# A decoder layer on one core: the pair's last norms in fewer slabs, their additions of squares on GpSimd, and half tiles and embedding weights stored two to a tile

## The chip, the core and the metric

The kernel runs on one core of a Trainium2 chip. The core has a matmul engine (PE, with its weight loads as PEld), a vector engine (DVE), a scalar engine (ACT), GpSimd (POOL) and a queue engine that issues most DMAs (SP). The metric is the device time of one execution in microseconds. The kernel before takes 1129.64 us (median of 3 runs, 1128.06 to 1129.97).

## The reference, cut to what matters

One layer of a decoder over 1,056 tokens (1,024 of a prompt and 32 samples), model width 1,024. What the change touches is the channel part, the last norm and the per-layer embedding:

```python
    x = x + _rms(mix, n_mix_post)
    f = _rms(x, n_ffn_pre)
    f = (jax.nn.silu(f @ w_gate) * (f @ w_up)) @ w_down
    x = x + _rms(f, n_ffn_post)
    x = x + jax.nn.sigmoid(x @ w_ple_gate) * (p @ w_ple)
```

`_rms` divides by the root of the mean square over the 1,024 features and multiplies by a gain. `w_gate` and `w_up` are 1,024 x 2,816, `w_ple` is 256 x 1,024. All is fp32.

## The kernel before

**Numbers and tokens.** Activations lie with the features on partitions and the tokens along a row. The 1,056 tokens form three groups of 352: groups 0 and 1 ("the pair") and group 2 ("the one"). Every fp32 operand is split in two: ACT casts the high part (L171), DVE subtracts it to get the low part (L172). A product is three matmuls (high by high, high by low, low by high; L126).

**The channel part.** It walks over 11 slabs of 256 hidden features, for the one and for the pair apart: six slabs for the one, eleven for the pair, then the last five for the one. For the one a weight tile takes 24 matmuls in one go (`direct`). For the pair, `seven` computes the two-by-two block product of a pair of weight tiles and the two groups with seven products of 12 matmuls rather than eight: it needs sums of the weights, made in place by four GpSimd operations of 128x512 (`w_sums`, L1012) and split like any weight into `sh`/`sl`, and sums of the activations, T1 to T4, each one GpSimd subtraction of 128x1408 (`t_sum`, L971). A slab's down products (6 matmuls each, `down`) are added on DVE to `o` (L1117), and run after the first gate product of the next slab.

**The end.** After the last slab of a group `last_down` also squares `o` on ACT and adds the squares up on DVE (`squares_into`, L802 and L803). `x2_steps` then makes the norm: a sum over partitions by matmuls with the reciprocal root (`rstd_steps`), the scaling (L1141), the gain and the residual (L1144), and the split of the result. For the pair `pair_steps` does this for groups 0 and 1, makes T1 to T4 from the results, and loads and splits the embedding input p of both groups (`pl_load`, L1156). The embedding then runs four pairs of output tiles (`ple_pair`), each a `seven` whose four results go through a sigmoid and are each followed by `embed`: 6 matmuls with `w_ple` and p, a product on DVE (L1212), an addition (L1214) and a DMA out. The down products of the one's last slab lie between the first pair and the second. Eight single output tiles of the one follow (`ple_one`, in the order `LATE`).

**What sets the order.** Each engine runs its instructions in the order of the program's list, and each instruction waits for what it needs. Two things are paced by hand. Weights are a list `ITEMS` in order of use; `need(k)` makes items up to four ahead: a DMA by SP into a ring of three raw tiles (`wr`), then a split into a ring of eight tiles (`wp`, shown as `wh`, `wl`, `sh`, `sl`). Kinds of items are "direct" (a whole tile), "half" (only the second half of a tile is needed as it is) and "sums" (the pair of tiles just loaded). The norms' steps are generators driven by `turn(n)`, called after n matmuls: a step yields (load, wait), and the next one is written into the program after `load / share` plus `wait` further matmuls. The chains of the pair and the one start at the end of `downs`.

**Names in the rows.** `b` is a PSUM bank (there are eight), `pl` the split p, `fh`/`fl` the split activations, `hid` the split hidden features, `a` the raw p, `x` the residual of a group with `x1d` and `x2d` its copies in DRAM, `xm` the residual read back for the embedding, `acc` the sum of squares, `yo` an output tile.

Of the kernel before, what the change touches and what calls it, by code (L numbers as in the profile page):

```python
# [61 lines left out]
def trunk_kernel(  # L62
# [167 lines left out]
    def direct_item(src, shape):  # L230
        return item("direct", add_plan(src, shape))

    def half_item(src):
        return item("half", add_plan(src, [P, KC, P]))
# [23 lines left out]
    for i in range(KC // 2):  # L258
        wp = direct_item(w_ple[i // 2], [P, 2, 512]) if i % 2 == 0 else WP2[-1][0]
        jg = direct_item(w_pg[2 * i], [P, KC, P])  # L260
        ju = half_item(w_pg[2 * i + 1])
        WP2.append((wp, jg, ju, item("sums", jg, ju)))
        if i == 0:
            WD[-1] = dn_items(len(WALK) - 1)
    LATE = (*range(4, KC), *range(4))
    for m in LATE:
        if m == 0:
            wp = direct_item(w_ple[0], [P, 2, 512])
        WPE[m] = wp, direct_item(w_pg[m], [P, KC, P])

    made = {}

    def need(k, ahead=LOOK):

        for i in range(len(made), min(k + ahead + 1, len(ITEMS))):
            kind, js = ITEMS[i]
            if kind == "direct":
                w_split(js[0])
                made[i] = pairs[js[0]]
            elif kind == "half":  # L280
                w_load(js[0])
                hl = w_tile([P, 4, P], "wh"), w_tile([P, 4, P], "wl")
                split(*hl, raws[js[0]][:, 4:8, :])
                made[i] = hl
            else:
                made[i] = w_sums(*(raws[ITEMS[j][1][0]] for j in js))
            for kind, js in ITEMS[i + 1 : i + 3]:
                if kind != "sums":
                    w_load(js[0])
        return made[k]  # L290
# [49 lines left out]

    def sum_halves(sqs, g):

        a, b = sqs
        fix(ve.tensor_tensor(a, a, b, op=ALU.add))
        fix(ve.tensor_tensor(a[:, 0:2, :], a[:, 0:2, :], a[:, 2:4, :], op=ALU.add))
        acc = acc_tile(g)
        fix(ve.tensor_tensor(acc, a[:, 0, :], a[:, 1, :], op=ALU.add))
        return acc
# [447 lines left out]

    def squares_into(acc_g, src, first):
        if first:
            se.activation(acc_g, src, AF.Square)
        else:  # L800
            sq = tmp(src.shape[-1], "sq")
            se.activation(sq, src, AF.Square)  # L802
            ve.tensor_tensor(acc_g, acc_g, sq, op=ALU.add)  # L803

# [110 lines left out]
    def ffn_steps(g):  # L915
# [7 lines left out]
        yield 0, 13  # L923
        acc2 = sum_halves(ys[g], g)
        yield 20, 6
        r = yield from rstd_steps(acc2)
# [200 lines left out]
    def last_down(n, m, g):  # L1127
        down(n, m, g)
        if m == 0:
            acc3[g] = acc_tile(g)  # L1130
        squares_into(acc3[g], os_[g][m // 4][:, m % 4, :], m == 0)

# [31 lines left out]
    def pair_steps():  # L1164
        for g in (0, 1):
            yield from x2_steps(g, pair_operand)
        for name in ("T1", "T2", "T4", "T3"):
            t_sum(name, x27, x2[0], x2[1], flat(os_))
            yield 20, 0
        for g in (0, 1):  # L1170
            pl_load(g)
            yield 6, 0

# [6 lines left out]
    def downs(n):  # L1180
# [6 lines left out]
        if n == LAST[0]:  # L1187
            share[0] = 0.35
            chain(pair_steps(), 19)
        if n == LAST[2]:  # L1190
            chain(one_steps(), 19)

# [11 lines left out]
    def embed(wp, xm, m, g, sg):  # L1204

        wh, wl = need(wp)
        ph, pl = pls[g]
        cols = slice((m % 4) * P, (m % 4 + 1) * P)
        pp = bank()
# [53 lines left out]
def _layout(i):  # L1263
# [29 lines left out]
        "w_pg": tiles(i["w_ple_gate"][0]),  # L1293
        "w_ple": i["w_ple"][0].reshape(2, P, 2, 512).transpose(2, 1, 0, 3),
        "gains": gains,
# [40 lines left out]
```

## Time and profile before

| | |
|---|---|
| median of 3 runs | 1129.64 us |
| the profiled execution | 1132.07 us, its span 1130.1 us, mean granted clock 0.992 |
| PE busy | 1105.7 us, 98% of the span |
| DVE busy | 828.6 us, 73% |
| ACT busy | 480.8 us, 43% |
| POOL busy | 233.1 us, 21% |
| DMA | 125.25 MB in packets, mean 111 GB/s |

The span is from the first instruction to the last; the execution's time lies 2 us above it. In the rows of an engine the first number is the start, the second the length, both in us, and in brackets stands how long the engine was idle before and what ended it. Matmuls are pipelined, so a row of 0.32 us starts every 0.16 us. In a table by stretches each engine has its busy time and, in brackets, its instructions; the granted clock is 1.00 at full speed.

The last stage of the profile in its chain of waits ends in one run of PE, and the outputs behind it:

```profile
1075.49 50.15 PE b L126 x304
1125.73 0.53 DVE sg L1212
1126.29 0.52 DVE yo L1214
```

### The profile page before, as it was taken

The page shows a single profiled execution, that of the slowest core. Times are in us where ns is not written, and L with a number is a line of the kernel's source. Part 1 is how long each engine was busy: PE and PEld are TensorE (multiplying, and loading weights), DVE is VectorE, ACT ScalarE, POOL GpSimd, SP SyncE. Part 2 cuts the span into 40 slices and gives each one's busy share as a digit, 9 for nine tenths or more (in the row PEclk, how much of TensorE's full clock was granted, in tenths as well). Part 3 has the DMA queues.
Part 4 walks back from the last instruction along what each step waited for, and adds up shares of the span by engine and source line. Part 5 has one row for each costly group of instructions (what it writes and reads, how often), then busy time and mean ns, then how long its engine had stood idle before and what let it go on. Part 6 is the DMA issues. An engine that isn't in the chain of part 4 may idle for free. (4 is left out here: it accounts for less than half of the span.)

```text
span 1130.1 us, 17901 instructions
## 1 busy us (share of the span) xinstructions
PE 1105.7 (98%) x7099; PEld 1088.3 (96%) x7099; DVE 828.6 (73%) x1314; ACT 480.8 (43%) x832; POOL 233.1 (21%) x180
## 2 busy tenths in 40 slices
PE   9999999999999999999999999999999999968998
PEld 8999988899999999999999999999999999968898
DVE  5767478877979966566767767767767888977763
ACT  6423277665645533523323323323325544534331
POOL 0045132100001413123123123122130001422400
PEclk9999999999999999999999999999999999989999
DMA  8121311642643422222222222212215355452451
GB/s 285 57 69 43 119 48 36 205 145 94 220 143 113 135 100 83 76 75 75 75 75 76 80 71 77 88 60 86 83 57 173 119 212 180 155 186 87 134 182 58
DMA packets 41844, 125.25 MB, mean 111 GB/s; under 512 B 4869, under 2 KB 15397, under 8 KB 41761
## 3 DMA queue, kind: packets, MB, share of 16 engines
q1 hardware_dynamic: 40432, 122.35, 32.0%
q10 hardware_dynamic: 1328, 1.77, 0.5%
q8 instruction: 56, 0.92, 0.3%
q14 instruction: 28, 0.22, 0.1%
HBM read 111.11 MB, written 12.99 MB: 110 GB/s over the span
## 5 line engine op out<-in xcount | busy, mean ns | idle before, releaser
L171 ACT CAST wh<-wr 128x1024 fp32r<-128x1024 f32 (+1 forms) x177 | 171.7, 971 | 254.9 <-PE b L126 182.1
L172 DVE TENSOR_TENSOR wl<-wr,wh 128x1024 fp32r<-128x1024 f32 (+1 forms) x177 | 214.5, 1218 | 65.2 <-ACT wh L171 59.5
L126 PE MATMUL b<-hid,wh 128*128 128x352 f32 x1056 | 252.1, 322 | 0.0
L126 PE MATMUL b<-fh,wh 128*128 128x352 f32 x728 | 236.1, 324 | 1.6 <-DVE o L1117 1.6
L126 PE MATMUL b<-fh,wl 128*128 128x352 f32 x728 | 234.0, 321 | 0.0
L126 PE MATMUL b<-fl,wh 128*128 128x352 f32 x728 | 234.0, 321 | 0.0
L126 PEld LDWEIGHTS b<-hid,wh 128*128 128x128 f32 x1056 | 182.5, 188 | 0.1
L126 PE MATMUL b<-hid,wl 128*128 128x352 f32 x528 | 169.1, 320 | 0.0
L1012 POOL TENSOR_TENSOR wr<-wr 128x512 f32<-128x512 f32 x52 | 70.8, 1362 | 412.6 <-DVE wl L172 385.6
L126 PEld LDWEIGHTS b<-fh,wh 128*128 128x128 f32 x728 | 137.3, 189 | 1.9 <-DVE o L1117 1.9
L126 PEld LDWEIGHTS b<-fl,wh 128*128 128x128 f32 x728 | 137.7, 189 | 0.0
L126 PE MATMUL b<-fh,sh 128*128 128x352 f32 x416 | 135.1, 325 | 2.3 <-ACT sh L171 2.3
L126 PEld LDWEIGHTS b<-fh,wl 128*128 128x128 f32 x728 | 137.0, 188 | 0.0
L126 PE MATMUL b<-fh,sl 128*128 128x352 f32 x416 | 134.1, 322 | 1.3 <-DVE sl L172 1.3
L126 PE MATMUL b<-fl,sh 128*128 128x352 f32 x416 | 133.9, 322 | 0.0
L1117 DVE TENSOR_TENSOR o<-o,b 128x352 f32<-128x352 f32 x240 | 112.4, 515 | 15.9 <-PE b L126 15.9
L126 PE MATMUL b<-h,wh 128*128 128x352 f32 x480 | 107.4, 330 | 1.0 <-ACT h L379 1.0
L172 DVE TENSOR_TENSOR sl<-wr,sh 128x1024 fp32r<-128x1024 f32 x52 | 63.5, 1222 | 56.1 <-ACT sh L171 56.1
L126 PEld LDWEIGHTS b<-hid,wl 128*128 128x128 f32 x528 | 98.9, 187 | 0.0
L171 ACT CAST sh<-wr 128x1024 fp32r<-128x1024 f32 x52 | 53.3, 1048 | 93.1 <-POOL wr L1012 67.8
L126 PEld LDWEIGHTS b<-h,wh 128*128 128x128 f32 x480 | 83.4, 192 | 2.5 <-ACT h L379 1.7
L126 PEld LDWEIGHTS b<-fh,sh 128*128 128x128 f32 x416 | 78.5, 189 | 2.9 <-ACT sh L171 2.9
(165 smaller groups left out, 1702.2 us busy)
## 6 DMA issues: line engine op xcount, KB each, us to landing
wr<-in_w_gu_dram SPq DMA_DIRECT2D x88, 512.0 KB, 3.2
wr<-in_w_dn_dram SPq DMA_DIRECT2D x44, 512.0 KB, 3.6
wr<-in_w_pg_dram SPq DMA_DIRECT2D x16, 512.0 KB, 3.8
x<-in_x_dram SPq DMA_DIRECT2D x6, 704.0 KB, 7.7
x1d<-x SPq DMA_DIRECT2D x6, 704.0 KB, 3.4
x<-x1d SPq DMA_DIRECT2D x6, 704.0 KB, 5.4
out_y_dram<-yo SPq DMA_DIRECT2D x24, 176.0 KB, 2.7
wr<-in_w_out_b_dram SPq DMA_DIRECT2D x8, 512.0 KB, 3.3
```

The source lines that it names most:

```text
L126: ins = te.matmul(*args, **kw)
L171: fix(se.copy(hi, src))
L172: fix(ve.tensor_tensor(lo, src, hi.bitcast(F32), op=ALU.subtract))
L1012: ge.tensor_tensor(out, a, b, op=op)
L1117: ve.tensor_tensor(o, o, v, op=ALU.add)
```

## The change

Four things change.

1. A half tile's two parts go into one `wp` tile (`two_in_one`), so a "half" item takes one place of the ring of eight and not two.
2. `w_ple` is laid out as four tiles of 256 columns, one for each pair of output tiles, not two of 512. Each is an item of the new kind "small", its two parts in one `wp` tile, and stands in `ITEMS` behind the pair's sums; before, it stood ahead of the pair's first weight, for two pairs at once. The one's tiles take them in the order 6, 7, 0 to 5, so that the last pair's can be used again.
3. `pair_steps` loads and splits p first and not last; the steps of T1 to T4 yield (15, 10) and not (20, 0); the pair's chain runs at share 0.5 and not 0.35 ("fewer slabs"); the one's chain starts after 40 matmuls and not 19.
4. The additions of squares in the last slab of the pair (14 of 128x352), and the three additions of `sum_halves` in the first norms of groups 0 and 1, go from DVE to GpSimd; the step behind `sum_halves` yields (0, 45) there.

PE has the same 6,856 instructions in both lists; DVE has 1,301 and not 1,317, ACT 781 and not 779, POOL 206 and not 186, SP 254 and not 250.

```diff
+    def small_item(src):
+        return item("small", add_plan(src, [P, 2, 256]))
...
-        wp = direct_item(w_ple[i // 2], [P, 2, 512]) if i % 2 == 0 else WP2[-1][0]
         jg = direct_item(w_pg[2 * i], [P, KC, P])
         ju = half_item(w_pg[2 * i + 1])
-        WP2.append((wp, jg, ju, item("sums", jg, ju)))
+        js = item("sums", jg, ju)
+        WP2.append((small_item(w_ple[i]), jg, ju, js))
...
-    LATE = (*range(4, KC), *range(4))
+    wp = WP2[-1][0]
+    LATE = (6, 7, *range(6))
     for m in LATE:
-        if m == 0:
-            wp = direct_item(w_ple[0], [P, 2, 512])
+        if m < 6 and m % 2 == 0:
+            wp = small_item(w_ple[m // 2])
...
+    def two_in_one(shape):
+        t = w_tile([P, 2, shape[1] * shape[2]], "w2")
+        return tuple(t[:, h, :].rearrange("p (a b) -> p a b", a=shape[1]) for h in range(2))
...
-                hl = w_tile([P, 4, P], "wh"), w_tile([P, 4, P], "wl")
+                hl = two_in_one([P, 4, P])
                 split(*hl, raws[js[0]][:, 4:8, :])
                 made[i] = hl
+            elif kind == "small":
+                w_load(js[0])
+                hl = two_in_one([P, 2, 256])
+                split(*hl, raws[js[0]])
+                made[i] = hl
...
-    def sum_halves(sqs, g):
+    def sum_halves(sqs, g, eng=ve):
...
-    def squares_into(acc_g, src, first):
+    def squares_into(acc_g, src, first, eng=ve):
...
-            ve.tensor_tensor(acc_g, acc_g, sq, op=ALU.add)
+            eng.tensor_tensor(acc_g, acc_g, sq, op=ALU.add)
...
-        acc2 = sum_halves(ys[g], g)
-        yield 20, 6
+        acc2 = sum_halves(ys[g], g, ve if g == 2 else ge)
+        yield (20, 6) if g == 2 else (0, 45)
...
-        squares_into(acc3[g], os_[g][m // 4][:, m % 4, :], m == 0)
+        squares_into(acc3[g], os_[g][m // 4][:, m % 4, :], m == 0, ve if g == 2 else ge)
...
     def pair_steps():
         for g in (0, 1):
+            pl_load(g)
+        for g in (0, 1):
             yield from x2_steps(g, pair_operand)
         for name in ("T1", "T2", "T4", "T3"):
             t_sum(name, x27, x2[0], x2[1], flat(os_))
-            yield 20, 0
-        for g in (0, 1):
-            pl_load(g)
-            yield 6, 0
+            yield 15, 10
...
-            share[0] = 0.35
+            share[0] = 0.5
             chain(pair_steps(), 19)
         if n == LAST[2]:
-            chain(one_steps(), 19)
+            chain(one_steps(), 40)
...
-        cols = slice((m % 4) * P, (m % 4 + 1) * P)
+        cols = slice((m % 2) * P, (m % 2 + 1) * P)
...
-        "w_ple": i["w_ple"][0].reshape(2, P, 2, 512).transpose(2, 1, 0, 3),
+        "w_ple": i["w_ple"][0].reshape(2, P, 4, 256).transpose(2, 1, 0, 3),
```

Three places of the order. First SP's queue, where the weights of the first embedding pair are asked for. Before (`in_p_dram` is p, `in_w_pg_dram` the gate weights of the embedding, `in_w_dn_dram` those of the down products):

```order
L181 DMA wr_9860<-in_w_ple_dram 128x1024
L181 DMA wr_9893<-in_w_pg_dram 128x1024
L181 DMA wr_9930<-in_w_pg_dram 128x1024
L181 DMA wr_10009<-in_w_dn_dram 128x1024
L1156 DMA a_10101<-in_p_dram 128x2x352
L1156 DMA a_10106<-in_p_dram 128x2x352
L181 DMA wr_10055<-in_w_dn_dram 128x1024
L181 DMA wr_10118<-in_w_pg_dram 128x1024
L1225 DMA xm_10110<-x2d_3023 128x1408
```

and changed:

```order
L181 DMA wr_9865<-in_w_pg_dram 128x1024
L181 DMA wr_9903<-in_w_pg_dram 128x1024
L181 DMA wr_9978<-in_w_ple_dram 128x512
L1237 DMA xm_10086<-x2d_3023 128x1408
L1237 DMA xm_10088<-x2d_3025 128x1408
L1150 DMA x_10451<-x1d_2535 128x1408
L1150 DMA x_10453<-x1d_2536 128x1408
L1237 DMA xm_10573<-x2d_3024 128x1408
L181 DMA wr_10024<-in_w_dn_dram 128x1024
```

The p tiles are gone from here (they are asked for some 30 DMAs earlier, in the pair's last slab), w_ple stands behind the pair's gate weights, and five loads of residuals stand ahead of the one's last down weights.

Second, DVE ahead of the first embedding pair, from the half split (128x512) to the first embed's product with p. Before:

```order
L172 TENSOR_TENSOR fl_10039<-o_4761,fh_10038 128x1408
L172 TENSOR_TENSOR fl_10087<-o_4796,fh_10086 128x1408
L172 TENSOR_TENSOR wl_10006<-wr_9930,wh_10005 128x512
L172 TENSOR_TENSOR fl_10092<-o_4762,fh_10091 128x1408
L1094 TENSOR_TENSOR sl_10011<-sl_10011,b_10057 128x352
L172 TENSOR_TENSOR fl_10097<-o_4795,fh_10096 128x1408
L172 TENSOR_TENSOR hid_9923<-sl_10011,hid_9923 128x352
L172 TENSOR_TENSOR sl_10048<-wr_9893,sh_10047 128x1024
L1041 TENSOR_TENSOR c_10141<-p_10126,b_10142 128x352
L172 TENSOR_TENSOR pl_10100<-a_10101,pl_10100 128x704
L172 TENSOR_TENSOR sl_10052<-wr_9930,sh_10051 128x1024
```

and changed:

```order
L1130 TENSOR_TENSOR o_3287<-o_3287,b_9996 128x352
L172 TENSOR_TENSOR w_9975<-wr_9903,w_9975 128x512
L1130 TENSOR_TENSOR o_3287<-o_3287,b_10004 128x352
L172 TENSOR_TENSOR sl_10017<-wr_9865,sh_10016 128x1024
L172 TENSOR_TENSOR sl_10021<-wr_9903,sh_10020 128x1024
L172 TENSOR_TENSOR w_10053<-wr_9978,w_10053 128x512
L1107 TENSOR_TENSOR sl_10026<-sl_10026,b_10058 128x352
L172 TENSOR_TENSOR hid_9931<-sl_10026,hid_9931 128x352
L1054 TENSOR_TENSOR c_10111<-p_10096,b_10112 128x352
```

The splits of T1 to T4 (`fl` from `o`, 128x1408) are no longer beside the half split, which is now `w_9975`; the split of p is gone; w_ple's split, `w_10053`, stands right behind those of the two sums.

Third, DVE where the splits of T1, T2 and T3 now stand, among the additions of a slab's down products (`o` and a bank):

```order
L172 TENSOR_TENSOR fl_9701<-x_9426,fh_9700 128x1408
L172 TENSOR_TENSOR wl_9634<-wr_9566,wh_9633 128x1024
L1107 TENSOR_TENSOR sl_9639<-sl_9639,b_9674 128x352
L172 TENSOR_TENSOR wl_9669<-wr_9600,wh_9668 128x1024
L172 TENSOR_TENSOR hid_9705<-sl_9639,hid_9705 128x352
L1130 TENSOR_TENSOR o_3286<-o_3286,b_9714 128x352
L1130 TENSOR_TENSOR o_3286<-o_3286,b_9722 128x352
L1130 TENSOR_TENSOR o_3286<-o_3286,b_9730 128x352
L172 TENSOR_TENSOR fl_9747<-o_4758,fh_9746 128x1408
L172 TENSOR_TENSOR wl_9709<-wr_9637,wh_9708 128x1024
L1130 TENSOR_TENSOR o_3286<-o_3286,b_9738 128x352
```

Before, T1's split stood further on, behind the additions of the slab after this one.

More of the change, by code (lines that the diff above doesn't have):

```diff
@@ L339, in acc_tile @@
         return spool.tile([P, NS[g]], F32, tag=f"acc{g}", bufs=1, name=nm("acc"))
-    def sum_halves(sqs, g):
+    def sum_halves(sqs, g, eng=ve):
         a, b = sqs
-        fix(ve.tensor_tensor(a, a, b, op=ALU.add))
-        fix(ve.tensor_tensor(a[:, 0:2, :], a[:, 0:2, :], a[:, 2:4, :], op=ALU.add))
+        fix(eng.tensor_tensor(a, a, b, op=ALU.add))
+        fix(eng.tensor_tensor(a[:, 0:2, :], a[:, 0:2, :], a[:, 2:4, :], op=ALU.add))
         acc = acc_tile(g)
-        fix(ve.tensor_tensor(acc, a[:, 0, :], a[:, 1, :], op=ALU.add))
+        fix(eng.tensor_tensor(acc, a[:, 0, :], a[:, 1, :], op=ALU.add))
         return acc
```

## The prediction

> **What bounds the kernel now.** I read the waits of PE first, then busy time by stage, then PE's own rows around each wait, and last the other engines' rows ahead of the longest one. The waits of the matmul engine (engine, line, what it waited for, total us, times, longest):
>
> ```profile
> PE b L126 <- ACT pl L171: 7.8, 1, 7.8
> PE b L126 <- DVE acc L803: 3.3, 1, 3.3
> PE b L126 <- ACT sh L171: 2.3, 2, 1.5
> PE b L126 <- DVE o L1117: 1.6, 1, 1.6
> PE b L126 <- DVE sl L172: 1.3, 2, 0.7
> PE b L126 <- DVE pl L172: 0.8, 1, 0.8
> ```
>
> The same execution by stretches (length, then PE's busy time and matmuls, PE's weight loads, DVE, ACT, POOL, the granted clock, DMA):
>
> ```profile
> 240.00:360.00 120.00, 118.40 (x749) 118.03 (x748) 97.23 (x135) 65.65 (x92) 3.23 (x1) 1.00 0.42 145
> 360.00:600.00 240.00, 240.00 (x1513) 240.00 (x1512) 171.47 (x249) 91.79 (x133) 65.67 (x43) 1.00 0.26 86
> 800.00:950.00 150.00, 150.00 (x948) 150.00 (x947) 114.68 (x181) 65.29 (x92) 16.17 (x12) 1.00 0.40 136
> 990.00:1080.00 90.00, 74.46 (x428) 72.35 (x427) 68.44 (x103) 36.59 (x52) 24.68 (x16) 0.91 0.41 136
> ```
>
> From 360 to 990 us PE has no idle time at full clock, 0.159 us a matmul (240 us / 1513). Nothing that shortens other engines' work there can show. All that can be won lies in 990 to 1080, the four pairs of the embedding. PE's rows there, and the one earlier wait (start, length, the idle time before it and what ended it):
>
> ```profile
> 355.99 0.43 PE L126 MATMUL b<-fh,wh 128*128 128x352 f32 x1 [1.60 <-DVE o L1117]
> 999.25 0.66 PE L126 MATMUL b<-pl,wh 128*128 128x352 f32 x1 [7.76 <-ACT pl L171]
> 1000.72 0.66 PE L126 MATMUL b<-pl,wh 128*128 128x352 f32 x1 [0.81 <-DVE pl L172]
> 1030.38 0.83 PE L126 MATMUL b<-c,acc 128*128 128x1 f32 x6 [3.28 <-DVE acc L803]
> 1054.79 0.43 PE L126 MATMUL b<-fh,sh 128*128 128x352 f32 x1 [1.52 <-ACT sh L171]
> 1056.05 0.43 PE L126 MATMUL b<-fh,sl 128*128 128x352 f32 x1 [0.67 <-DVE sl L172]
> 1074.23 0.43 PE L126 MATMUL b<-fh,sh 128*128 128x352 f32 x1 [0.83 <-ACT sh L171]
> 1075.49 0.51 PE L126 MATMUL b<-fh,sl 128*128 128x352 f32 x1 [0.67 <-DVE sl L172]
> ```
>
> The last seven sum to 15.54 us. The clock adds to it:
>
> ```profile
> 1000.00:1005.00 5.00, 4.28 (x17) 4.29 (x18) 3.12 (x4) 2.59 (x4) 0.00 (x0) 0.60 0.77 262
> 1030.00:1035.00 5.00, 4.62 (x21) 4.62 (x22) 4.38 (x10) 3.64 (x5) 0.00 (x0) 0.66 0.65 211
> 1055.00:1060.00 5.00, 4.33 (x26) 4.04 (x26) 5.00 (x7) 2.37 (x4) 0.00 (x0) 1.00 0.57 174
> 1075.00:1080.00 5.00, 4.51 (x18) 4.51 (x19) 4.97 (x8) 1.81 (x3) 0.00 (x0) 0.66 0.71 188
> ```
>
> A busy 5 us at full clock holds 31 matmuls. After the 7.76 wait 17 take 4.28 us instead of 2.7, and the slow stretch begins before 1000, so I put its loss at 2.3; in the stretches with 0.66, after 3.28 and after 0.83 + 0.67, the loss is 1.7 each (18 in 4.51 instead of 2.86). After 1.52 + 0.67 the clock stays at 1.00. So 5.7 us of clock belong to three of the four stalls, and 15.5 + 5.7 = 21.2 us is all that this change can remove here.
>
> Why was pl late at 999? The rows of POOL, DVE, ACT and SP's queue before it:
>
> ```profile
> 989.04 2.61 POOL L1012 TENSOR_TENSOR wr<-wr 128x512 f32<-128x512 f32 x1 [14.09 <-DVE wl L172]
> 995.83 1.26 POOL L1012 TENSOR_TENSOR wr<-wr 128x512 f32<-128x512 f32 x1
> 985.21 3.15 DVE L172 TENSOR_TENSOR fl<-o,fh 128x1408 fp32r<-128x1408 f32 x2
> 988.28 0.68 DVE L172 TENSOR_TENSOR wl<-wr,wh 128x512 fp32r<-128x512 f32 x1
> 998.20 1.23 DVE L172 TENSOR_TENSOR sl<-wr,sh 128x1024 fp32r<-128x1024 f32 x1 [3.57 <-ACT sh L171]
> 997.12 1.04 ACT L171 CAST sh<-wr 128x1024 fp32r<-128x1024 f32 x1 [5.67 <-POOL wr L1012]
> 998.42 0.78 ACT L171 CAST pl<-a 128x704 fp32r<-128x704 f32 x1
> 982.88 4.58 SPq L1156 DMA_DIRECT2D a<-in_p_dram  x2
> ```
>
> The p rows are asked for at 982.88, last in the norms' chain, but ACT's cast of them stands behind `sh`, which waits for the weight sums on POOL. Those start at 989.04 because DVE's half split came behind two `fl` splits. So two things are late, and the second matters: had `pl` alone been early, the sums' `sl` would still have been ready only at 999.43. A forecast has to place the sums too.
>
> **The change, part by part.** The changed order fixes which instruction waits for which; times come from the rows. I count matmuls to the end of the program: 702 remain after the last matmul before the 7.76 stall (end 991.5).
>
> *p first.* Both p DMAs, ACT casts (0.78 us each) and DVE splits move some 100 us earlier, between 870 and 880, where PE is full (150 of 150) and DVE has 35 us to spare in 150. SP's queue passes two more DMAs there and two fewer at 983. Price nothing; without that cover two splits, about 0.8 us each.
>
> *Norms earlier.* In the order, group 1's norm takes its matmuls 116 matmuls (18 us) earlier, so T2, T4, T3 on POOL start about 945 and not 963, and their splits no longer stand ahead of the first half split. That split waits for the last down but one (775 matmuls left, 979.9 us), so sums can run 981.3 to 987 instead of 989 to 997.1, with `sh` at 988 and `sl` at 989.2 and 990.7. Gain here: 7.76 + 0.81 + 2.3 = 10.9.
>
> The price is where the T sums land. These are the rows of POOL and DVE where they run now:
>
> ```profile
> 963.32 3.97 POOL L971 TENSOR_TENSOR o<-x,o 128x1408 f32<-128x1408 f32 x1 [7.72 <-DVE x L1144]
> 967.25 4.23 POOL L971 TENSOR_TENSOR o<-x,x 128x1408 f32<-128x1408 f32 x1
> 971.44 3.51 POOL L971 TENSOR_TENSOR o<-x,o 128x1408 f32<-128x1408 f32 x1
> 962.98 1.21 DVE L172 TENSOR_TENSOR wl<-wr,wh 128x1024 fp32r<-128x1024 f32 x1
> 965.75 2.63 DVE L172 TENSOR_TENSOR wl<-wr,wh 128x1024 fp32r<-128x1024 f32 x1 [0.33 <-ACT wh L171]
> 968.30 3.56 DVE L172 TENSOR_TENSOR hid<-sl,hid 128x352 fp32r<-128x352 f32 x1
> 971.78 4.25 DVE L172 TENSOR_TENSOR wl<-wr,wh 128x1024 fp32r<-128x1024 f32 x1
> ```
>
> A DVE split that reads two SBUF tiles ends only after the POOL subtraction beside it: 4.25 instead of 1.21. Now most of this falls between two batches of down products. In the new order it falls on one: eight downs fill the eight banks (966 to 918 matmuls left, 949.5 to 957.1 us), and the DVE addition that empties the first stands behind `fl`, two `wl` and `hid`, each able to wait for one POOL subtraction. Bounds: 0, if the queue clears in time; 4.1, if DVE is held for all 11.7 us of the three (3.97 + 4.23 + 3.51) against 7.6 us of banks, or 5.8 with 1.7 of clock. I take 2.4, nearest to the 1.60 at 355.99, which is this same collision with one subtraction.
>
> The Trainium skill, "SBUF — State Buffer", section "Who interferes with whom", states that a VectorE instruction with two SBUF inputs and a GpSimd instruction that reads SBUF exclude each other for the whole instruction; the rows above agree (4.25 us against 1.21), and it speaks against putting more additions on GpSimd.
>
> *Squares and half sums on GpSimd.* 14 additions of 128x352 and six of `sum_halves` leave DVE (1317 instructions become 1301). The trace has no such addition on POOL; its 128x512 one takes 1.26 us undisturbed (995.83), so I scale 0.9 us, and a down product's six matmuls run 0.95 us: POOL keeps step. Bounds: no gain, since PE is full there; at worst 14 x 0.9 = 12.6 us of DVE held, against 35 spare, so no loss either. The half sums lie at 300 to 320, where PE's one wait from 240 to 360 is the 1.60 of T1, which I let stand; bounds there -1.6 (it goes) to +3.2 (one more such wait for each group). Taken: 0.
>
> *Half tiles and the embedding's weights two to a tile.* In the loop a slab takes 18 ring tiles, not 20: weights come no earlier than PE can use them, 0. In the embedding, w_ple of each pair is now split after both sums, and the pair's first embed product needs it. Before, that product waited for no sums; now split, sums, both `sh` and `sl` and w_ple's own split must fit into the matmuls between the half tile's release and that product. I measure the chain by the third and the first pair of now (DVE's rows):
>
> ```profile
> 1000.58 1.22 DVE L172 TENSOR_TENSOR sl<-wr,sh 128x1024 fp32r<-128x1024 f32 x1
> 1046.24 0.68 DVE L172 TENSOR_TENSOR wl<-wr,wh 128x512 fp32r<-128x512 f32 x1
> 1054.77 2.36 DVE L172 TENSOR_TENSOR sl<-wr,sh 128x1024 fp32r<-128x1024 f32 x2 [4.13 <-ACT sh L171]
> ```
>
> Half split to the end of the second `sl` takes 10.9 us (1046.24 to 1057.13) to 13.5 (988.28 to 1001.80); with a cast ahead and w_ple's split behind it, each about 0.65, 12.2 to 14.8.
>
> - First pair: 73 matmuls, 11.6 us. Short by 0.6 to 3.2; the lower end, 0.7, since little else is queued on DVE there.
> - Second: 78 matmuls, 12.4 us. Short by 0 to 2.4, but DVE also has five additions of downs and six of squares (11, about 0.45 us each) between, so up to 7.4; stepped through in order, 3.6, which is near the 3.28 whose clock loss was 1.7. Taken 5.3. It takes the place of group 2's norm wait (3.28 + 1.7 = 5.0), which now comes 18 matmuls later.
> - Third: two us of slack, 0, so 1.52 + 0.67 = 2.2 goes.
> - Fourth: short by 0 to 3.2, taken 0.9; with half of a 1.7 clock loss 1.8. The old 0.83 + 0.67 + 1.7 = 3.2 goes.
>
> The Trainium skill, "TensorE: Matmul & The Clock Gate", section "What's actually happening", gives an idle window of about 3.4 us as what halves the clock; the 7.76 and 3.28 us waits bear that out roughly, the 0.66 after 0.83 + 0.67 does not. By the page the fourth pair would lose 0.9 and not 1.8.
>
> The eight single products of the tail wait for nothing in either order.
>
> **Sum.** Gone: 10.9 + 5.0 + 2.2 + 3.2, the 21.2 of above but for rounding. New: 2.4 + 0.7 + 5.3 + 1.8 = 10.2. Net -11.0 us. The profiled execution took 1132.07 us (span 1130.1, 2.0 around it), 2.4 above the median of 1129.64; its own forecast is 1121.1, and against the median **1118.6**.
>
> **The rivals.**
>
> - *All stalls go.* If the T sums clear the queue and the second pair's squares wait behind the sums' `sl`, new waits are 0 to 5, 16 to 21 are gained: about 1110. For it: POOL is idle from 971.44 + 3.51 to 989.04. Against: every pair's embed now needs the sums.
> - *The stall is only handed on.* If the half split is again behind DVE's long splits by 5 us, the first pair waits 5 + 1.7 in place of 10.9, and the rest comes as above: 11 - 6 = 5 gained, 1124.6. For it: the row 998.20, the sums late by themselves. Against: in the order only the `fl` of T4 remains ahead.
> - *Slower: sums on every pair's path.* One mechanism: DVE, held by POOL, hands the half tile over late, and w_ple's split, now behind the sums, stops PE in each pair. At the upper bounds: 5.8 at the T sums, 3.2 + 2.3 in the first pair, 7.4 + 1.7 in the second, 3.2 + 1.7 in the third and in the fourth, 30.2 against 21.2: 1138.6; halfway between its threshold and that, 1134. It decides once the new waits exceed 21.2. The port rule named above would be its cause. For it: 2.61 us at 989.04 for a POOL sum that takes 1.26 at 995.83. Against: all bounds must meet.
> - *Nothing moves.* The norms' pace changes but PE finds the same waits, 1129.6. Against it stands the order, where p and group 1's norm do move.
>
> **How the numbers follow.** Forecast 0.5 (own range 1115 to 1122), all stalls go 0.18, handed on 0.17, slower 0.12, nothing 0.03. A measurement of this kernel tells about 0.2%, 2.3 us, from no change. Faster: 0.5 + 0.18 + 0.16 = 0.84; same: 0.03 + 0.01 and 0.01 of the slower case = 0.05; slower 0.11. The range 1109 to 1128 takes in the forecast, most of the second case and the third, and leaves out the slower one.
>
> **What will show it.** PE's wait for `pl` is gone, and POOL's first sums of the embedding start near 981; POOL's T sums run at 945 to 957, with a PE wait of 2 to 3 us for an `o` addition near 957; the first embed product of the second pair waits 3 to 4 us for the two-in-one tile near 1017; PE stays full from 360 to 945. Wrong it is if the first sums start after 986, if PE waits between 870 and 945 for POOL's additions, or if the third pair waits too.

## The result and the profile after

| | median | lowest to highest | runs |
|---|---|---|---|
| before, in the same rounds | 1129.6 us | 1128.06 to 1133.12 | 14 |
| changed | 1119.99 us | 1118.06 to 1128.1 | 14 |

The ratio is 0.9915, with a 95% interval of 0.9901 to 0.993: the change takes 9.6 us off (7.9 to 11.2). The profiled execution of the changed kernel took 1120.06 us (span 1117.9, mean clock 0.997), at its median; that of before lay 2.4 above its own.

Busy time by engine in the changed kernel (us, share of the span, instructions):

```profile
PE 1102.0 (99%) x7099; PEld 1084.3 (97%) x7099; DVE 818.8 (73%) x1298; ACT 476.6 (43%) x834; POOL 259.7 (23%) x200
```

PE is busy 3.7 us less than before at the same work, with a mean clock of 0.997 for 0.992. All its waits of 0.1 us and more from 200 us on are these (start, length, idle time before it and what ended it):

```profile
351.21 0.59 PE L126 MATMUL b<-hid,wh 128*128 128x352 f32 x2 [0.42 <-DVE o L1130]
352.79 0.43 PE L126 MATMUL b<-fh,wh 128*128 128x352 f32 x1 [0.34 <-DVE o L1130]
370.33 0.43 PE L126 MATMUL b<-hid,wh 128*128 128x352 f32 x1 [1.17 <-DVE hid L172]
957.75 0.43 PE L126 MATMUL b<-fh,wh 128*128 128x352 f32 x1 [2.16 <-DVE o L1130]
1021.25 0.59 PE L126 MATMUL b<-pl,w 128*128 128x352 f32 x2 [2.16 <-ACT w L171]
1022.83 1.28 PE L126 MATMUL b<-pl,w 128*128 128x352 f32 x4 [0.98 <-DVE w L172]
1033.26 0.40 PE L126 MATMUL b<-dg,c 128*128 128x352 f32 x1 [0.61 <-DVE dg L340]
1034.71 0.43 PE L126 MATMUL b<-dg,c 128*128 128x352 f32 x1 [1.05 <-DVE dg L340]
```

They sum to 8.89 us, where before had 17.14 (1.60 and the seven of 15.54). The waits for `pl`, for `acc`, and for `sh` and `sl` of the third and the fourth pair are all gone. Three new places have come: 957 (the T sums), 1021 (`w`, the two-in-one tile of w_ple for the second pair) and 1033 (`dg`, a diagonal tile made of the reciprocal root in the one's norm). The wait of 1.60 at 355 has become three, up to 370.

The stretches around them, with columns as before (length, PE, PEld, DVE, ACT, POOL, clock, DMA):

```profile
800.00:950.00 150.00, 150.00 (x948) 150.00 (x947) 116.44 (x173) 67.46 (x94) 40.96 (x29) 1.00 0.44 149
955.00:965.00 10.00, 7.84 (x39) 7.55 (x38) 10.00 (x14) 5.70 (x6) 0.74 (x1) 0.83 0.33 118
990.00:1080.00 90.00, 85.20 (x519) 83.86 (x519) 76.81 (x119) 41.56 (x62) 16.34 (x12) 0.98 0.40 134
1020.00:1030.00 10.00, 7.76 (x39) 7.47 (x40) 6.60 (x12) 4.96 (x8) 1.28 (x1) 0.83 0.29 97
```

From 990 to 1080 PE does 519 matmuls where it did 428. After the waits at 957 and 1021 the clock falls to 0.83: 39 matmuls there take 7.84 and 7.76 us instead of 6.2 (39 x 0.159), so in this execution each wait costs some 1.6 us more than itself. Eight of the kernels below have this wait too (2.16 to 2.19 us, at 956 to 965), and in each of their profiles the clock stays at 1.00 behind it; so the 1.6 at 957 can't be put down to the change.

What is behind the three new waits shows in the other engines' rows. First GpSimd: three of the four T sums (L984), the weight sums of the first pair (983.98) and those of the third (1028.67):

```profile
943.75 3.23 POOL L984 TENSOR_TENSOR o<-x,o 128x1408 f32<-128x1408 f32 x1 [5.54 <-DVE x L1157]
946.95 4.61 POOL L984 TENSOR_TENSOR o<-x,x 128x1408 f32<-128x1408 f32 x1
951.52 4.22 POOL L984 TENSOR_TENSOR o<-x,o 128x1408 f32<-128x1408 f32 x1
...
983.98 1.29 POOL L1025 TENSOR_TENSOR wr<-wr 128x512 f32<-128x512 f32 x1 [28.23 <-DVE w L172]
...
1028.67 1.28 POOL L1025 TENSOR_TENSOR wr<-wr 128x512 f32<-128x512 f32 x1 [14.31 <-DVE w L172]
1030.04 2.67 POOL L1025 TENSOR_TENSOR wr<-wr,wr 128x512 f32<-128x512 f32 x2
```

Then DVE at the same times:

```profile
944.96 3.51 DVE L172 TENSOR_TENSOR fl<-x,fh 128x1408 fp32r<-128x1408 f32 x1 [1.44 <-ACT fh L171]
948.39 4.24 DVE L172 TENSOR_TENSOR wl<-wr,wh 128x1024 fp32r<-128x1024 f32 x1
...
952.99 3.83 DVE L172 TENSOR_TENSOR wl<-wr,wh 128x1024 fp32r<-128x1024 f32 x1
956.75 0.51 DVE L172 TENSOR_TENSOR hid<-sl,hid 128x352 fp32r<-128x352 f32 x1
957.18 1.37 DVE L1130 TENSOR_TENSOR o<-o,b 128x352 f32<-128x352 f32 x3
...
1015.47 1.23 DVE L172 TENSOR_TENSOR sl<-wr,sh 128x1024 fp32r<-128x1024 f32 x1 [3.21 <-ACT sh L171]
...
1020.52 1.22 DVE L172 TENSOR_TENSOR sl<-wr,sh 128x1024 fp32r<-128x1024 f32 x1
1021.65 0.52 DVE L816 TENSOR_TENSOR acc<-acc,sq 128x352 f32<-128x352 f32 x1
1022.09 0.69 DVE L172 TENSOR_TENSOR w<-wr,w 128x512 fp32r<-128x512 f32 x1
...
1031.46 3.19 DVE L340 TENSOR_TENSOR dg<-c,hl 128x384 fp32r<-128x384 f32 x2
```

At 944 to 957 three splits of 1.2 to 1.6 us last 3.5 to 4.2 beside the subtractions, and the addition of `o` that frees a bank for PE comes at 957.18. Between the first `sl` of the second pair (1015.47) and the second (1020.52) DVE makes five additions of squares of group 2 and four of its last downs; one more addition of squares follows, and only then, at 1022.09, w_ple's split, which ends the second wait (0.98). The first and longer one (2.16) ends with ACT's cast of w_ple, which stands behind the squares of the same downs:

```profile
1020.20 0.50 ACT L815 ACTIVATE sq<-o 128x352 f32<-128x352 f32 x1 [0.31 <-DVE o L1130]
1020.60 0.60 ACT L171 CAST w<-wr 128x512 fp32r<-128x512 f32 x1
```

At 1031.46 two `dg` take 3.19 us while POOL makes the third pair's weight sums; the same two took 1.02 in group 1's norm at 923.27, with nothing beside them.

### The profile page after: what moved, and what is told of

The parts are those of the page before. It is cut to its first block, busy times and chain, and to the rows that moved or that the text cites. A ratio compares the mean times of both kernels' runs of the same rounds, so it can differ in the third digit from the quotient of the medians.

```text
span 1117.9 us, 18031 instructions
## 1 busy us (share of the span) xinstructions
PE 1102.0 (99%) x7099; PEld 1084.3 (97%) x7099; DVE 818.8 (73%) x1298; ACT 476.6 (43%) x834; POOL 259.7 (23%) x200
## 4 chain that ended last, share of the span: by engine, by line
PE 93%; DVE 4%; DMA 2%; POOL 1%; issue 1%; ACT 0%; SPq 0%; DVEq 0%; POOLq 0%; ACTq 0%
PE b L126 92%; DVE wl L172 1%; PE b L120 1%; DMA a<-in_dmask_dram 1%; POOL wr L1025 0%; DVE fl L172 0%; DVE hid L172 0%; DMA xr<-in_x_dram 0%; DMA wr<-in_w_gu_dram 0%; DVE dg L340 0%; DVE acc L816 0%; DVE mx L659 0%; DVE a L767 0%; DVE o L1130 0%; DVE y L944 0%
## 5 line engine op out<-in xcount | busy, mean ns | idle before, releaser
L172 DVE TENSOR_TENSOR wl<-wr,wh 128x1024 fp32r<-128x1024 f32 (+1 forms) x148 | 195.7, 1323 | 43.5 <-ACT wh L171 33.6
L171 ACT CAST wh<-wr 128x1024 fp32r<-128x1024 f32 (+1 forms) x148 | 152.4, 1031 | 159.0 <-PE b L126 108.7
L126 PE MATMUL b<-fh,wh 128*128 128x352 f32 x624 | 202.7, 325 | 2.5 <-DVE o L1130 2.5
L126 PE MATMUL b<-fh,wl 128*128 128x352 f32 x624 | 201.2, 322 | 0.0
L126 PE MATMUL b<-fl,wh 128*128 128x352 f32 x624 | 201.0, 322 | 0.0
L1025 POOL TENSOR_TENSOR wr<-wr 128x512 f32<-128x512 f32 x52 | 67.8, 1303 | 431.2 <-DVE w L172 373.7
L126 PEld LDWEIGHTS b<-fh,wh 128*128 128x128 f32 x624 | 117.7, 189 | 3.1 <-DVE o L1130 3.1
L126 PEld LDWEIGHTS b<-fl,wh 128*128 128x128 f32 x624 | 118.1, 189 | 0.0
L126 PEld LDWEIGHTS b<-fh,wl 128*128 128x128 f32 x624 | 117.8, 189 | 0.0
L171 ACT CAST sh<-wr 128x1024 fp32r<-128x1024 f32 x52 | 54.2, 1045 | 131.3 <-POOL wr L1025 129.9
L126 PEld LDWEIGHTS b<-fl,sh 128*128 128x128 f32 x416 | 78.2, 188 | 0.0
```

What stands on the lines that cost most here:

```text
L126: ins = te.matmul(*args, **kw)
L171: fix(se.copy(hi, src))
L172: fix(ve.tensor_tensor(lo, src, hi.bitcast(F32), op=ALU.subtract))
L1025: ge.tensor_tensor(out, a, b, op=op)
```

## The experiments

The theory was that of the prediction: the norms' earlier place frees DVE and GpSimd, so that p and the weight sums both come in time; the T sums and w_ple behind the sums give half of it back. The rivals: p alone was late; or the additions on GpSimd or the ring's places are what matters. The table has every kernel, the sum of PE's waits of 0.1 us or more from 200 to 1115 us in its profile, and the ratio to before in the same rounds. The medians of before were 1129.68 (beside e1 to e4), 1129.99 (e5 to e8) and 1130.37 (e9 to e12). The expectations call the kernels by the short names in brackets.

| kernel | median us | ratio (95%) | waits of PE, us |
|---|---|---|---|
| before | 1129.6 | | 17.14 |
| changed | 1119.99 | 0.9915 (0.9901 to 0.993) | 8.89 |
| before, p first (e1) | 1124.91 | 0.9954 (0.9939 to 0.997) | 12.23 |
| before, the whole pace (e2) | 1116.85 | 0.9877 (0.9854 to 0.9899) | 7.00 |
| the pace and p first (e3) | 1116.57 | 0.9883 (0.9856 to 0.991) | 5.95 |
| changed, additions on DVE (e4) | 1118.4 | 0.9909 (0.9875 to 0.9942) | 8.75 |
| changed, w_ple ahead of the pair (e5) | 1120.2 | 0.9922 (0.9905 to 0.9939) | 9.20 |
| changed, two tiles for each half (e6) | 1132.85 | 1.0027 (1.0013 to 1.0041) | 17.40 |
| pace, p first, two-in-one, w_ple ahead (e7) | 1118.4 | 0.9899 (0.9886 to 0.9912) | 8.42 |
| the same, T sums of the embedding on DVE (e8) | 1115.68 | 0.9877 (0.9864 to 0.989) | 6.51 |
| pace, p first, additions on GpSimd (e9) | 1117.63 | 0.9879 (0.9859 to 0.99) | 6.46 |
| before, share 0.5 alone (e10) | 1122.23 | 0.9926 (0.99 to 0.9952) | 10.99 |
| pace, p first, embedding's T sums on DVE (e11) | 1113.26 | 0.9856 (0.9829 to 0.9883) | 4.09 |
| the same, the channel part's T1 too (e12) | 1110.53 | 0.9821 (0.9799 to 0.9843) | 4.10 |

The time follows the sum of the waits in nearly every row, with the lowered clock behind some waits on top.

**p first, alone.** In before:

```diff
     def pair_steps():
+        for g in (0, 1):
+            pl_load(g)
         ...
-        for g in (0, 1):
-            pl_load(g)
-            yield 6, 0
```

> The kernel before, with p of groups 0 and 1 loaded and split at the start of the pair's last norms; nothing else of the change. Theory (two things were late, p and the weight sums): the wait for pl of 7.76 + 0.81 us goes, but PE then stops three products later for the sums' sh and sl, about 4 us and 1 us, with the clock loss that follows; 3 to 5 us faster, 1125 to 1127 us. Rival (pl alone was what PE waited for): the whole 10.9 us go, 1119 us. The POOL sums still start near 989.

It took 1124.91 us, 4.7 less than before, just under the 1125 to 1127 that I expected and far from the 1119 of the rival. PE's row at the first pair:

```profile
999.59 0.43 PE L126 MATMUL b<-fh,sh 128*128 128x352 f32 x1 [3.90 <-ACT sh L171]
```

and what that `sh` waited for, on DVE (the two splits of T sums, the half split, then `sl`):

```profile
986.55 3.15 DVE L172 TENSOR_TENSOR fl<-o,fh 128x1408 fp32r<-128x1408 f32 x2
989.62 0.68 DVE L172 TENSOR_TENSOR wl<-wr,wh 128x512 fp32r<-128x512 f32 x1
...
999.57 1.22 DVE L172 TENSOR_TENSOR sl<-wr,sh 128x1024 fp32r<-128x1024 f32 x1 [3.57 <-ACT sh L171]
```

p is early, and the sums are late by themselves: the half split still stands behind two `fl`, and `sl` begins at 999.57.

**The pace, with p still last; then both.** In before:

```diff
-            yield 20, 0
+            yield 15, 10
-            share[0] = 0.35
+            share[0] = 0.5
-            chain(one_steps(), 19)
+            chain(one_steps(), 40)
```

> The kernel before with the pair's norms paced as in the change (share 0.5, the T sums yield 15 and 10, the one's chain after 40 matmuls), and p still last in the chain; no p first, no additions on GpSimd, no two-in-one tiles. Theory (the pace makes both the sums and p early enough): no wait of more than 2 us at the first embedding pair, a new wait of 1.5 to 3 us for an o addition at 918 matmuls before the end; 1120 to 1124 us. Rival (p's place in the chain decides): a wait for pl of over 4 us stays, 1126 us or more.

> e2 with p first as well: the third part of the change alone, without GpSimd additions, two-in-one tiles and the w_ple items behind the sums. Theory (this part carries nearly the whole gain, and the rest moves waits from the third and fourth pair to the second): 1119 to 1123 us, within 2 us of e2, with waits at sh and sl in the third and fourth pair as before (3 to 4 us in sum) and under 1 us at the second pair's first embed. Rival (the tiles two to a ring place are needed to make the sums early): 1125 us or more.

The pace alone gives 1116.85: more than the whole change, and more than I expected. With p first it is 1116.57, no difference that shows. Both lie below the stretches that I had given (1120 to 1124, 1119 to 1123). The pace brings p forward too, since the chain that loads it ends sooner: SP asks for it at 974.93 and not at 982.88. GpSimd's first weight sum and ACT's cast of p in the kernel with the pace alone:

```profile
986.32 1.29 POOL L1012 TENSOR_TENSOR wr<-wr 128x512 f32<-128x512 f32 x1 [31.57 <-DMA xm<-x2d]
```

```profile
980.54 0.78 ACT L171 CAST pl<-a 128x704 fp32r<-128x704 f32 x1 [3.45 <-DMA a<-in_p_dram]
```

In before that cast was at 998.42. So the gain of the change is that of its pace, p's new place adds nothing that shows, and parts 1, 2 and 4 take back what lies between 1116.57 and 1119.99. The two intervals just overlap (0.9856 to 0.991, 0.9901 to 0.993), that of the pace alone (to 0.9899) lies apart; the waits, 5.95 and 8.89 us, say the same.

**One number of it.** Before with `share[0] = 0.5` and nothing else.

> The kernel before with one number changed: the pair's chain at share 0.5 in place of 0.35. Theory (this number brings the T sums and their splits ahead of the half split, which removes the first pair's wait; the one's chain after 40 matmuls removes group 2's norm wait of 3.28): first pair under 2 us of waits, the wait for acc of about 3.3 us stays with its clock loss; 1118.5 to 1121.5 us. Rival (the pieces of the pace only work together): a wait of over 4 us at the first pair, 1124 us or more.

1122.23, just above the expected stretch: this one number takes off 8.1 us of the 13.1 of the pace and p first together. What the steps' (15, 10) and the later start of the one's chain give each for itself wasn't run. The wait for the one's norm, `acc`, is still there with 3.41 us; with the whole pace it is 0.83, and with p first too it is gone.

**The additions back on DVE.** In the changed kernel:

```diff
-        acc2 = sum_halves(ys[g], g, ve if g == 2 else ge)
-        yield (20, 6) if g == 2 else (0, 45)
+        acc2 = sum_halves(ys[g], g)
+        yield 20, 6
-        squares_into(..., m == 0, ve if g == 2 else ge)
+        squares_into(..., m == 0)
```

> The changed kernel with the additions of squares and the half sums of groups 0 and 1 back on DVE, the step behind them yielding 20 and 6 as before. Theory (they lie where PE is full): 1119 to 1121.5 us, PE full from 600 to 945. Rival 1 (GpSimd's reads hold up DVE): faster than the changed kernel by over 1.5 us. Rival 2 (DVE needs the relief to make group 1's norm early): slower by over 1.5 us, T sums later than in the changed kernel.

> e3 (p first and the pace) with the change's additions on GpSimd and their yields; no two-in-one tiles, w_ple as before. Theory (the additions themselves lie where PE is full; only the half sums shift the first norms, 1.9 us of waits at 350 to 370 against 1.6): 1116.6 to 1118.5 us, PE full from 600 to 945. Rival (GpSimd's additions hold DVE up, as e4's 1.6 us suggests, or more): over 1118.5 us, with waits between 870 and 945.

1118.4, which is 1.6 less than changed, below the 1119 to 1121.5 that I expected and just past the line that I had drawn for rival 1; but two of its six runs took 1125.86 and 1126.83, and its interval (0.9875 to 0.9942) takes in that of the changed kernel. And the other way round, the additions put on GpSimd in the kernel with the pace and p first, 1117.63, as expected, which is 1.1 more. Each is near what a measurement tells from nothing; both have the same sign. In the profile of the second PE is full from 600 to 945 us:

```profile
600.00:945.00 345.00, 345.00 (x2175) 345.00 (x2175) 259.32 (x403) 130.90 (x188) 85.08 (x63) 1.00 0.32 107
```

so the 14 squares cost nothing there. The half sums and the later step behind them turn the one wait of 1.60 at 355 into three, of 0.41, 0.36 and 1.34 us. Half a microsecond of the loss is seen that way. The waits show no more: those of changed and of changed with the additions on DVE differ by 0.14 us in sum (8.89 and 8.75), and the lower clock behind 957, 1.6 us, is one execution's. Rival 1 is neither shown nor ruled out.

**Two tiles for each half tile, as before.** In the changed kernel, w_ple still behind the sums:

```diff
     def two_in_one(shape):
-        t = w_tile([P, 2, shape[1] * shape[2]], "w2")
-        return tuple(t[:, h, :].rearrange("p (a b) -> p a b", a=shape[1]) for h in range(2))
+        return w_tile(shape, "wh"), w_tile(shape, "wl")
```

> The changed kernel with half tiles and w_ple items as two tiles of the ring again; w_ple still behind the sums. Theory (one ring place instead of two releases the half split and w_ple's split earlier; without it w_ple's split waits for the last matmul before the embed): waits for w of over 1 us at the first embed of all four pairs, 1122 to 1127 us. Rival (ring places do not matter there): 1119 to 1121 us.

1132.85, slower than before, and by more than I expected. PE's waits grouped (total, times, longest):

```profile
PE b L126 <- ACT wh L171: 8.8, 4, 3.1
PE b L126 <- DVE wl L172: 4.5, 3, 1.7
```

`wh` and `wl` are here the two parts of w_ple: the first product with p waits in all four pairs. What the slower rival of the prediction fears comes true here, w_ple's split stopping PE in each pair, though not by its cause: this kernel differs from the changed one only in the ring's places, and not in what GpSimd does. Once w_ple stands behind the sums, every pair's embedding needs the sums, and the ring's places decide whether they come in time. The two-in-one tile is what makes w_ple's place bearable; no run shows a gain of it by itself.

**w_ple ahead of the pair's first weight.** In the changed kernel (e5), and in the changed kernel with the additions back on DVE (e7):

```diff
+        jp = small_item(w_ple[i])
         jg = direct_item(w_pg[2 * i], [P, KC, P])
         ju = half_item(w_pg[2 * i + 1])
         js = item("sums", jg, ju)
-        WP2.append((small_item(w_ple[i]), jg, ju, js))
+        WP2.append((jp, jg, ju, js))
```

> The changed kernel with each pair's w_ple item ahead of the pair's first gate weight instead of behind its sums; else as changed. Theory (only this order makes the second pair's first embed wait for the sums): the waits of 2.16 and 0.98 us for w at 546 matmuls before the end go, and with the third pair's sums later, so do the waits for dg of 0.61 and 1.05; 1114 to 1117 us. Rival (the sums' chain of the second pair is late by itself): a wait of over 2 us moves to the products with sh or sl behind it; 1118 us or more.

> The change without its GpSimd additions and with w_ple ahead of the pair: the pace, p first and the two-in-one tiles only. Theory: e3's waits of 0.94 and 0.67 for sh and sl in the third pair go, since the half split comes 18 matmuls earlier, and no new ones come; 1113.5 to 1116 us, at or below e3's 1116.6. Rival (the ring places gained are worth nothing): as e3, 1116.6 us with the same waits.

Both missed: 1120.2 where I expected 1114 to 1117, and 1118.4 where I expected 1113.5 to 1116. The waits for w_ple and for `dg` are gone as meant, but others came in their place (9.20 and 8.42 us in all). The longest, 2.78 us, is in the fourth pair of the second kernel; PE, then DVE:

```profile
1061.93 0.40 PE L126 MATMUL b<-fh,sh 128*128 128x352 f32 x1 [2.78 <-DVE p L1055]
```

```profile
1052.43 2.52 DVE L172 TENSOR_TENSOR fl<-x,fh 128x1408 fp32r<-128x1408 f32 x1
...
1060.13 1.22 DVE L172 TENSOR_TENSOR sl<-wr,sh 128x1024 fp32r<-128x1024 f32 x1 [3.63 <-ACT sh L171]
1061.27 0.51 DVE L1055 TENSOR_TENSOR p<-p,b 128x352 f32<-128x352 f32 x1
```

DVE idles 3.63 us for the sums, with the addition of a product of `seven` (`p`, L1055) next behind `sl`; PE waits for the bank that this addition empties. In the kernel with the pace and p first, where w_ple is laid out as before, the same two come the other way round, and the addition is done before the sums are waited for:

```profile
1053.40 0.51 DVE L1041 TENSOR_TENSOR p<-p,b 128x352 f32<-128x352 f32 x1
...
1054.70 2.28 DVE L172 TENSOR_TENSOR fl<-x,fh 128x1408 fp32r<-128x1408 f32 x1
1059.24 1.23 DVE L172 TENSOR_TENSOR sl<-wr,sh 128x1024 fp32r<-128x1024 f32 x1 [2.26 <-ACT sh L171]
```

My expectation had taken away a wait and not asked what the new list puts behind the sums.

**The T sums on DVE.** These ask whether GpSimd's subtractions are what PE waits for at 957 and at 355. `t_sum` gets an engine, and only the calls differ: in the kernel with two-in-one tiles and w_ple ahead, and in the one with the pace and p first, the four sums of the embedding; then T1 of the channel part as well.

```diff
-            t_sum(name, x27, x2[0], x2[1], flat(os_))
+            t_sum(name, x27, x2[0], x2[1], flat(os_), ve)
...
-t_sum("T1", f7, ys[0], ys[1], flat(ys))
+t_sum("T1", f7, ys[0], ys[1], flat(ys), ve)
```

> e7 with the four T sums of the embedding on DVE instead of GpSimd. Theory (the wait of 2.2 us for an o addition near 957 comes from GpSimd's subtractions holding up DVE's splits, 4.2 us instead of 1.2): DVE takes 1.6 us for each sum, but its splits take 1.2 again, and the wait falls under 1 us; 2 us less than e7, 1111 to 1114 us. Rival (DVE is short of time there in any case): the wait stays at 2 us or grows, e7's time or more.

> e3 with the four T sums of the embedding on DVE. Theory (as e8 showed: the wait of 2.2 us near 957 is GpSimd holding up DVE's splits): that wait goes, nothing new comes; 1113.5 to 1115.5 us, faster than both kernels. Rival (the time comes back later as in e8, where waits of 2.78 and 1.3 us stood in the pairs): 1116.6 us or more.

> e11 with T1 of the channel part (at about 351 us) on DVE as well. Theory (the wait of 1.6 us at 355, one subtraction of GpSimd holding up one split, is the same thing): that wait falls under 0.6 us; 1 to 1.6 us less than e11. Rival (eight full banks decide it, whichever engine subtracts): 1.6 us stay, e11's time.

1115.68 (2.7 less than without, but above the 1111 to 1114 that I expected), 1113.26 (3.3 less, just under the expected 1113.5) and 1110.53 (2.7 less again, where I had expected at most 1.6). The first and the third ran beside the kernel that they are compared with, and no run of the one reaches the other's; the second didn't, and its interval overlaps that of the kernel without (0.9829 to 0.9883, 0.9856 to 0.991), so there the rows carry the argument. DVE in the second of these, where the subtractions (L971) now are:

```profile
943.15 1.62 DVE L971 TENSOR_TENSOR o<-x,x 128x1408 f32<-128x1408 f32 x1
944.69 1.62 DVE L172 TENSOR_TENSOR fl<-x,fh 128x1408 fp32r<-128x1408 f32 x1
946.23 1.22 DVE L172 TENSOR_TENSOR wl<-wr,wh 128x1024 fp32r<-128x1024 f32 x1
947.36 1.62 DVE L971 TENSOR_TENSOR o<-x,o 128x1408 f32<-128x1408 f32 x1
```

and the stretches of the third, around the old waits at 355 and 957:

```profile
240.00:360.00 120.00, 120.00 (x761) 119.91 (x760) 97.22 (x137) 65.37 (x91) 0.00 (x0) 1.00 0.44 149
940.00:990.00 50.00, 50.00 (x317) 50.00 (x316) 39.82 (x49) 23.70 (x28) 5.14 (x4) 1.00 0.58 208
```

DVE does a subtraction in 1.62 us that takes GpSimd 3.2 when it starts ahead of a split (943.75) and over 4 when it starts beside one (946.95), and no split is held (1.22 and 1.62, not 4.24 and 3.51). PE is full in both stretches. The last kernel, before with the pace, p first and these sums on DVE, beats both: 19.8 us under before and 9.5 under the changed one by their medians, and its range (1109.97 to 1111.99) lies below every other kernel's. With w_ple in the old layout and no two-in-one tiles it is also the smaller edit.

The rows bear out what the prediction drew from the Trainium skill, "SBUF — State Buffer", section "Who interferes with whom", that a VectorE instruction with two SBUF inputs and a reading GpSimd instruction hold each other off: taking GpSimd's side away brings each split back to 1.22 or 1.62 us.

## Why the prediction was right, and where it was not

The forecast of 1118.6 was 1.4 us under the median, inside its own range of 1115 to 1122 and nearer than the interval of the gain is wide. Step by step:

- **All that can be won lies in the four pairs.** Right for this change. What can be won in all was more: the last experiment takes away T1's wait at 355, which the sum let stand, and is 2.7 us faster.
- **Two things are late, and p early would leave `sl` at 999.43.** Shown by p first alone: `sl` begins at 999.57 and is ready at 1000.79, and PE waits 3.90 us for the sums.
- **First pair, 10.9 gone, 0.7 new.** Gone, and there is no new wait. The first weight sum starts at 983.98 and not 981.3; the 981.3 was counted without the new wait at 957.
- **T sums, 2.4.** The mechanism is as written (`fl`, `wl`, `wl`, `hid`, then the addition) and is shown by taking GpSimd out of it. It measured 2.16 us of wait. In this execution the clock adds 1.6, which I had counted only at the upper bound; in the eight other profiles with this wait it adds nothing, so the 2.4 is nearer to what most profiles show than the 3.8.
- **p first, 0.** It costs nothing. I had priced its gain together with the sums' and never asked what it adds to the pace: nothing that shows.
- **Squares and half sums on GpSimd, 0.** A loss of 1.1 to 1.6 by the medians, near what can be told from nothing and within the bounds given. The squares cost nothing under a full PE; the wait of T1, which I had let stand, became three with 0.3 us more in the changed kernel. The last of them, 1.17 at 370, lies in the stretch that was to stay full (360 to 945), so this sign failed by that much. An addition of 128x352 takes 0.95 us on GpSimd (873.66), for my 0.9.
- **Ring places, 0.** In the loop nothing shows. In the embedding the step was priced with w_ple's move; two tiles for each half, with w_ple behind the sums, cost 12.9 us.
- **Second pair, 3.6 and 1.7 of clock.** 2.16 + 0.98 = 3.14 of wait and 1.6 of clock: 4.7 for 5.3. Third pair: no wait for its sums, as forecast. Fourth pair: 1.8 forecast, 0 measured; the lower bound was the right one.
- **What I did not see.** The 1.66 us for `dg`. I had asked of POOL's sums only which splits they hold. In the changed kernel the third pair's sums start at 1028.67, just ahead of the one's two `dg`, and these are held in the same way. It is w_ple's place that brings the sums so early, and not the later start of the one's norm: with the pace and p first the norm starts as late, the sums come at 1032.73, and the `dg` take 1.02; with w_ple ahead they take 1.02 as well.

New terms by these rows: 3.8 + 4.7 + 1.66 + 0.3 = 10.5, for 10.2 in the sum. That they agree so closely is luck: two terms that did not come (0.7, 1.8) cancel one that was missing and the clock of one execution. The two profiled executions lie 12.0 us apart, but 2.6 of that arise ahead of everything that changed (the last section shows the rows), so 9.4 are the change's, for 10.7 by the terms (21.2 - 10.5); the 1.3 us between them aren't located. Against the medians the sum gave 11.0 and 9.6 came, which the interval of 7.9 to 11.2 does not tell apart.

Of the rivals, "handed on" did not come: the half split is no longer behind the T sums' splits. What the slower one fears is real, since two tiles for each half bring it, but in the change the two-in-one tiles keep it to the second pair. None of the three signs of being wrong came: the first sums start ahead of 986, PE does not wait between 870 and 945, and the third pair does not wait.

What stays open: where the rest of the 1.1 to 1.6 us of the additions goes, if it is more than noise, and what lies behind the 1.3 us above. That T1 on DVE gave 2.7 where its wait was 1.59 can be followed in the two profiles, which lie 2.3 apart. At the wait for `acc`, 0.44 us in both, the last kernel is 2.36 ahead (1015.35 for 1017.71), of which 1.59 is the wait and 0.5 an earlier start. Behind it nothing more is won: its waits are 1.6 longer (3.66 for 2.06), and the clock stays at 1.00, where the other loses some 1.7 from 1036 to 1046 (42 matmuls in 8.48 us). So 1.6 of the 2.7 are shown.

## What to carry to other kernels

When two things are late at one place, take them apart by one kernel each: here the pace alone was worth more than the whole change, and the parts added to it took some of that back. Before work goes to a second engine to relieve the first, read what the two do to each other while they overlap: DVE had room for the T sums, and with them on DVE, in half the time, the kernel was 3.3 and 2.7 us faster. When a wait is taken away by moving an item in an in-order queue, list what then stands behind it; two such expectations missed here, by 3.2 and 2.4 us beyond their upper ends.

## What the runs showed of the hardware that was not expected

- **The clock after a short wait.** Waits of the same length at the same place end differently. Of the nine profiles with a wait of 2.16 to 2.19 us for the T sums only the changed kernel's shows a lower clock behind it, 0.83 from 955 to 965 (39 matmuls). In the kernel with the pace it stays at 1.00, its row for the same stretch being

```profile
955.00:965.00 10.00, 8.24 (x52) 8.24 (x53) 10.00 (x15) 5.18 (x6) 0.00 (x0) 1.00 0.40 127
```

The Trainium skill, "TensorE: Matmul & The Clock Gate", section "What's actually happening", has the gate close after an idle window of about 3.4 us that runs freely. Both waits are shorter, so that threshold alone does not tell which of them is followed by a lower clock. Still shorter waits are followed by one too: 0.94 + 0.67 us in the third pair with the pace and p first by 0.66 (1040 to 1045), 0.95 + 0.67 at the same place in the last kernel by none. A loss of 1.6 us in one profile is therefore not yet a cost of the wait ahead of it.
- **Small DVE instructions are held too.** Two `dg` of 128x384 took 3.19 us beside a GpSimd sum and 1.02 without; the cast of 128x3 just ahead of them took 0.88 and not 0.17.
- **The start of a stage moves by some us between executions.** The same group of matmuls, ahead of everything that changes, comes in before and in the changed kernel at

```profile
218.95 1.04 PE L120 MATMUL b<-c,a 128*128 128x128 f32 x8
216.38 1.03 PE L120 MATMUL b<-c,a 128*128 128x128 f32 x8
```

In the other profiles it lies between 216.05 and 217.54, but for one at 218.92. The late start would account for the 2.4 us by which the profiled execution of before lies above its median.
- **The pace of a matmul at full clock differs between executions.** From 500 to 800 us, with the granted clock at 1.00 and no wait, PE does 1,890 or 1,891 matmuls in twelve of the profiles, 1,877 with p first alone and 1,864 in the changed kernel with w_ple ahead. The profiled executions of these two lie 4.5 and 5.4 us above their medians (1129.43 for 1124.91, 1125.63 for 1120.2), so their profiles serve for the waits and not for the time.
